# A hybrid encoder block on one core: the second copy of the keys made in the memory-attention stage, and five units instead of seven woven with the grouped-query attention

## The chip, the core and the metric

The kernel runs on one core of a Trainium2 chip. The metric is device time in microseconds, the median over runs. The engines are named as in the profile: PE is TensorE's matrix multiplication and PEld its weight load, DVE is VectorE, ACT is ScalarE, POOL is GpSimd, SP is SyncE, which here only issues transfers. "PSUM bank" is one of the eight accumulators of 128 x 512 float32 that matmuls write to; SBUF is the on-chip memory of 128 partitions.

## The reference, cut to what matters

One sub-layer with three mixers side by side. All inputs are float32, 1024 tokens, width 1024.

```python
h = rms_norm(x, g_pre[layer])
a_qkv, bq, bk, bv, mq, ga, gb, gm, mg = jnp.split(h @ w_in[layer], split_at, axis=-1)
# 1. dilated window attention: 3 groups of 8 heads, merged by their log-denominators -> oa
# 2. grouped-query attention: 8 query heads, 2 key heads of width 64
qb_ = axial_rope(rms_norm(bq, q_norm), row_pos, col_pos)
kb_ = axial_rope(rms_norm(bk, k_norm), row_pos, col_pos)
sc = jnp.einsum('bqkgd,bskd->bkgqs', qc, kb_).astype(jnp.float32) * (HEAD_DIM ** -0.5)
p = jax.nn.softmax(sc, axis=-1)
ob = jnp.einsum('bkgqs,bskd->bqkgd', p, vb_)
# 3. cross-attention of 4 heads of width 128 into a memory of 256 tokens -> om
ya = (oa * jax.nn.silu(ga)) @ w_br_a[layer]
yb = (ob * jax.nn.silu(gb)) @ w_br_b[layer]
ym = (om * jax.nn.silu(gm)) @ w_br_m[layer]
gates = jax.nn.sigmoid(mg + b_merge[layer])   # 3 x 1024 columns of the same h @ w_in
merged = gates[:, :, 0] * ya + gates[:, :, 1] * yb + gates[:, :, 2] * ym
x = x + rms_norm(merged @ w_out[layer], g_post[layer])
```

## The kernel before

**Precision and units.** A float32 product is made of three matmuls in a rounded float32 format: each operand is split into a high and a low part (`split`, lines 104 to 106: ACT writes the high part, DVE the remainder), and high x high, low x high and high x low are summed in PSUM. The normalised input stands in SBUF as `hh[k]`, `hl[k]` for eight blocks of 128 input channels. The columns of `w_in` that give transposed outputs are cut into units of 128: `add_unit` (line 195) queues one, `load_w` (line 110) loads its 512 KB of weights on SP and splits them, and `dense` (line 139) runs 2 halves x 8 channel blocks x 3 = 48 matmuls of 128 x 512 (lines 143, 145, 147). What is done with the result differs: `add_gate` (line 216) makes a SiLU gate of a branch and stores it to `g2d`; `add_filler` (line 207) makes tanh of one of the 24 merge-gate units and stores it to `thd`.

**Weaving.** The order on PE is written out: `weave` (line 174) alternates the matmuls of queued units with the pieces of an attention generator, in proportion to the costs that both announce with `yield`. While an item runs, the next one is prepared (weights loaded and split). On ACT, DVE, POOL and SP the tile scheduler chooses the order in most stages, by priority and by when its own model thinks operands are ready; each engine then runs its list strictly in that order. `tc.issue_after(x)` keeps an instruction behind another one.

**The stages in order of time.** Loading and splitting the input, keys and values of the grouped-query branch; memory keys and values; the memory-attention stage (`m_att`, about 98 to 217 us), woven with the query projection (`b_q`), the four memory-query units and one gate unit; the grouped-query stage (`b_att`, 217 to 462 us), woven with the units that this change counts; the values of the window attention in seven block products; the window attention (592 to about 1003 us), woven with its own query and key units and four gate units (`GATES_A`); the block stage (1011 to 1220 us), in which the remaining merge-gate units are made in pairs; then the three branch products and the output.

**The grouped-query stage.** `KS` holds the two key heads transposed, key on 64 rows, high part in rows 0 to 63 and low part in rows 64 to 127. `QH` holds the queries' high part in both halves, so `KS` x `QH` over 128 rows gives high x high and low x high at once. The third product takes `QL`, the queries' low part in rows 0 to 63 and, in rows 64 to 67, the row maximum of one of four heads on a diagonal; its partner is `KB`: the keys' high part again in rows 0 to 63 and -1 in rows 64 to 67, so the same matmul subtracts the maximum. The steps, for 8 query blocks x 2 key heads = 16 rounds of 8 steps:

- `q_prep` (line 661), every second round: four transposes of the normalised queries into one PSUM bank, four ACT copies to `QH`, two DVE subtractions to `QL`, which release the bank.
- `row_max` (line 713), one a step: a matmul of 128 x 512 and a DVE reduction (line 721). Its banks, three of them, also serve `q_prep`, `shift` and `final`.
- `shift` (line 725): the maxima transposed and put into `QL` (DVE, line 729).
- `scores` (line 732), 12 steps behind `row_max`: two matmuls (738 and 739), the exponential on ACT (741), the running sum of denominators on POOL (743, 745).
- `pv` (line 748), once a round, 14 steps behind: 16 matmuls with the values (754), ACT and DVE evacuations (756, 757), and the split of the finished sum into `lh`, `ll` (the profile calls them `blh`, `bll`).
- `final` (line 760), 15 steps behind: two matmuls of a column of ones with `blh` and `bll`, copied out by ACT (766) and stored.

`b_const` (line 683) is called in step 1: it makes `KB` and clears two small tiles. `token_block` (692), in steps 18, 42, 66 and 90, prepares sums of input blocks for later stages.

The woven units are the gate units (2,3) and (1,0) to (1,3), five, and `FILL_B = (16, 17)`, two merge-gate units. Line 823 prepares the first value weights for the next stage behind the last unit.

**The block stage.** `rest` (line 1344) lists the merge-gate units that are not in `FILL_B`, in the order 16 to 23, 8 to 15, 0 to 7, and `pairs` takes them by two: 11 pairs before. A pair is a 2 x 2 block product made with seven products instead of eight (`PRODUCTS`, line 1426), each 4 x 3 = 12 matmuls of 128 x 512: 84 for a pair, where two units alone have 96. `slot` (line 1528) puts the other engines' work behind each product, among it the five steps of `combine` for the last head pair, at products of pairs 0 to 4 (`COM`, line 1526); results are stored to `thd` from the ACT queue (line 1466). `last` is the number of the last pair, and the loads for the branch products count from it.

**SBUF.** `KS` and the values lie in a pool that lives through both attention stages; `QN`, the queries, in pool `qn`, opened before the memory-attention stage and closed after the grouped-query one. `mt` holds the memory attention's tiles and `ba` those of the grouped-query stage; both begin behind `qn`. A tile that reuses memory waits for the last user of the tile that lay there.

Of the kernel before, what the change touches and what calls it, by code (L numbers as in the profile page):

```python
# [8 lines left out]
F32 = mybir.dt.float32  # L9
R = mybir.dt.float32r  # L10
AF = mybir.ActivationFunctionType
# [4 lines left out]
S = 1024  # L16
NT = 8
P = 128
# [32 lines left out]
def block(ctx: ExitStack, tc: tile.TileContext, x, xT, memT, cst, msk, bcst, tabA, gpost,  # L51
          wu, wv, wb, wmem, wbr, wout, out):
    nc = tc.nc
    V, A, G, PE = nc.vector, nc.scalar, nc.gpsimd, nc.tensor
# [24 lines left out]
    def pss1():  # L79
        return bank["p"].tile([P, 512], F32, name="s1", tag="s1", bufs=bank["n"][1])  # L80

    def pst():
        return bank["p"].tile([P, 4, 128], F32, name="tr", tag="t", bufs=bank["n"][2])

    def pso():
        return bank["p"].tile([P, 512], F32, name="ov", tag="o", bufs=bank["n"][3])
# [6 lines left out]
    ones = const.tile([P, 1], F32, name="ones")  # L93
# [10 lines left out]
    def split(dst_h, dst_l, src):  # L104
        A.activation(dst_h, src, AF.Copy)  # L105
        V.tensor_tensor(dst_l, src, dst_h.bitcast(F32), op=OP.subtract)  # L106
# [3 lines left out]
    def load_w(src, n=1024):  # L110
        if extra:
            extra.append(extra.pop(0))
        raw = (extra[0] if extra else wp).tile([P, 1024], F32, name="wr", bufs=WR)
        nc.sync.dma_start(raw[:, :n], src)
        wh = wp.tile([P, 1024], R, name="wh")
        wl = wp.tile([P, 1024], R, name="wl")
        split(wh[:, :n], wl[:, :n], raw[:, :n])
        k = n // 128
        return (wh[:, :n].rearrange("p (k f) -> p k f", k=k),
                wl[:, :n].rearrange("p (k f) -> p k f", k=k))  # L120

    def passes(out_ps, terms):
        n = len(terms)
        for i, (a, b) in enumerate(terms):
            PE.matmul(out_ps, a, b, start=i == 0, stop=i == n - 1)  # L125
# [37 lines left out]
    def run_items(count):  # L163
        for _ in range(count):
            n = done[0]
            prepare(n)
            prepare(n + 1)
            yield from queue[n][1](ready.pop(n))
            done[0] += 1

    def cost_items(count):
        return sum(q[2] for q in queue[done[0]:done[0] + count])

    def weave(count, att=None, att_cost=0.0, lead=1.0, prio=ATT_PRIO):
        dg = run_items(count)
        dc = cost_items(count)
        d = a = 0.0
        live_d, live_a = True, att is not None
        while live_d or live_a:
            if live_d and (not live_a or a / att_cost >= min(1.0, d / dc * lead)):  # L180
                try:
                    d += next(dg)
                except StopIteration:
                    live_d = False
                    d = 1e18
            else:
                try:
                    with tc.high_priority(offset=prio):
                        a += next(att)
                except StopIteration:  # L190
                    live_a = False
# [11 lines left out]
    fp = {}  # L203
# [32 lines left out]
    def pool(name, side="left"):  # L236
        p = tc.tile_pool(name=name, bufs=1, side=side, reuse_waits="tile")
        return p, p.__enter__()
# [8 lines left out]
    KS = kvl.tile([P, 2, S], R, name="KS")  # L247
# [50 lines left out]
    def proj_tok(w, T, dst):  # L298
        th, tl = w
        t = slice(T * 128, T * 128 + 128)  # L300
        for k in range(8):
            PE.matmul(dst, hh[k][:, t], th[:, k], start=k == 0, stop=False)
            yield 109
            PE.matmul(dst, hl[k][:, t], th[:, k], start=False, stop=False)
            yield 109
            PE.matmul(dst, hh[k][:, t], tl[:, k], start=False, stop=k == 7)
            yield 109
# [122 lines left out]
    def b_q(c, w):  # L430
        for T in range(NT):
            p = psd() if T % 2 else pss1()
            yield from proj_tok(w, T, p[:, 0:256])
            qk_norm_rope(p, 4, T, tabs["Cq"], tabs["Sq"], -0.125, QN[T][:, 4 * c:4 * c + 4])

# [125 lines left out]

    qp, ql_ = pool("qn")
    QN = [ql_.tile([P, 8, 64], F32, name=f"qn{T}") for T in range(NT)]
    mtp, mt_ = pool("mt")
    fp["p"] = mt_

    def m_att(h):
        qh, ql = MQ[h]
        for _ in range(4):
            yield 250  # L570
        st = {}

        def scores(n):
            sv = pss1().rearrange("p (t k) -> p t k", t=2)
            nm = mt_.tile([P, 2], F32, name="mnm", bufs=3)
            l = mt_.tile([P, 2], F32, name="mls", bufs=3)
            pm = mt_.tile([P, 2, 256], F32, name="pm", bufs=2)
            for j in range(2):
                t = slice((2 * n + j) * 128, (2 * n + j) * 128 + 128)
                passes(sv[:, j], [(qh[:, t], kmh[:, h]), (qh[:, t], kml[:, h]), (ql[:, t], kmh[:, h])])  # L580
            V.tensor_reduce(nm, sv, axis=AX.X, op=OP.min)
            V.tensor_tensor(nm, nm, rcol[:, 2 * n:2 * n + 2], op=OP.mult)
            for j in range(2):
                A.activation(pm[:, j], sv[:, j], AF.Exp, scale=nrcol[:, 2 * n + j:2 * n + j + 1], bias=nm[:, j:j + 1],
                             accum_out=l[:, j:j + 1])
            rl = mt_.tile([P, 2], F32, name="mrl", bufs=4)
            V.reciprocal(rl, l)
            for j in range(2):
                V.tensor_scalar(pm[:, j], pm[:, j], rl[:, j:j + 1], None, op0=OP.mult)
            st[n] = pm  # L590

        def trans(n):
            pm = st[n]
            tp = pst().rearrange("p (k t) q -> p k t q", k=2)
            for kt in range(2):
                for j in range(2):
                    PE.transpose(tp[:, kt, j, :], pm[:, j, kt * 128:kt * 128 + 128], ident)
            ph = mt_.tile([P, 2, 256], R, name="mph", bufs=2)
            pl = mt_.tile([P, 2, 256], R, name="mpl", bufs=2)
            split(ph, pl, tp.rearrange("p k t q -> p k (t q)"))  # L600
            st[n] = (ph, pl)

        def pv(n):
            ph, pl = st.pop(n)
            o = pso()
            terms = []
            for kt in range(2):
                terms += [(vmh[:, kt, h], ph[:, kt]), (vmh[:, kt, h], pl[:, kt]), (vml[:, kt, h], ph[:, kt])]
            passes(o[:, 0:256], terms)
            om = mt_.tile([P, 256], F32, name="om", bufs=2)  # L610
            A.activation(om, o[:, 0:256], AF.Copy)
            nc.sync.dma_start(od[2, h, :, n * 256:n * 256 + 256], om)

        for n in range(7):
            if n < 4:
                scores(n)
            yield 654
            if 0 <= n - 2 < 4:
                trans(n - 2)
            yield 436  # L620
            if 0 <= n - 3 < 4:
                pv(n - 3)
            yield 654
# [7 lines left out]
    add_gate(2, 2)  # L631
    early[len(queue)] = lambda: load_w(wu[U_G + 11])
    weave(1)
    weave(2, m_att(0), M_COST, 1.2)
    weave(2, m_att(1), M_COST, 1.2)
    weave(1, m_att(2), M_COST, 1.0)
# [20 lines left out]
    with tc.tile_pool(name="ba", bufs=1, reuse_waits="tile") as ba:  # L657
# [3 lines left out]
        def q_prep(T):  # L661
# [4 lines left out]
            for j in range(4):  # L666
                PE.transpose(tp[:, j, :], QN[T][:, 2 * j:2 * j + 2].rearrange("p a b -> p (a b)"), ident)
            for e in range(2):
# [4 lines left out]
                a = slice(e * 64, e * 64 + 64)  # L673
                V.tensor_tensor(QL[0:64, e], tp[a], QH[a, e].bitcast(F32), op=OP.subtract)

        KB = ba.tile([P, 2, S], R, name="KB")
        QQ[0] = (ba.tile([P, 8, 128], R, name="QH", bufs=2), ba.tile([P, 8, 128], R, name="QL", bufs=2))
        lh = ba.tile([P, 512], R, name="blh")
        ll = ba.tile([P, 512], R, name="bll")
# [1 line left out]
        one = ba.tile([P, 1], R, name="one")  # L681
        nmt = [ba.tile([P, 68], F32, name=f"bnm{i}") for i in range(2)]
        def b_const():
            with tc.issue_after(fp["copy"].ins):
                A.activation(KB[64:68], ones[64:68, :, None].to_broadcast([4, 2, S]), AF.Copy, scale=-1.0)
            with tc.issue_after(fp["last"].ins):
                V.tensor_copy(KB[0:64], KS[0:64].bitcast(F32))
            G.tensor_copy(one, ones)
            for t in nmt:
                V.memset(t, 0.0)  # L690
# [18 lines left out]
        def b_att():  # L709
# [22 lines left out]
            def scores(i, kt):  # L732
# [5 lines left out]
                PE.matmul(s, KS[:, kv, t], QH[:, h], start=True, stop=False)  # L738
                PE.matmul(s, KB[0:68, kv, t], QL[0:68, h], start=False, stop=True)  # L739
                pp = ba.tile([P, 512], F32, name="bp", bufs=BP)  # L740
# [74 lines left out]
        for i in (2, 1, 0):  # L815
            for p_ in range(4):
                if (i, p_) not in ((2, 0), (2, 1), (2, 2)) + GATES_A:
                    add_gate(i, p_)
                    ng += 1
        for j in FILL_B:  # L820
            add_filler(j)
# [198 lines left out]
    with tc.tile_pool(name="aa", bufs=1, reuse_waits="tile") as aa:  # L1020
# [322 lines left out]

        rest = [j for i in (2, 1, 0) for j in range(8 * i, 8 * i + 8) if j not in FILL_B]
        pairs = list(zip(rest[::2], rest[1::2]))
# [43 lines left out]
        for n in range(len(seq)):  # L1389
# [6 lines left out]
            last = n + 1 == len(seq)  # L1396
# [30 lines left out]
    last = len(pairs) - 1  # L1427
# [318 lines left out]
G_AT = 4  # L1746
ATT_PRIO = 120
LA_T, LA_P = 2, 3
FILL_B = (16, 17)
GATES_A = ((0, 0), (0, 1), (0, 2), (0, 3))  # L1750
VG = (2, 0, 1)
U_G = 24
# [107 lines left out]
```

## Time and profile before

| | us |
|---|---|
| median of 3 runs (1448.71, 1448.78, 1450.25) | 1448.78 |
| the profiled execution, by the device's own time | 1449.86 |
| its span, from first to last instruction | 1448.1 |
| grouped-query stage, first row maximum to the next stage's first matmul | 245 |
| TensorE's granted clock, mean | 0.998 |

The page's first part gives the busy time of each engine, its share of the span and its number of instructions. Views by stretch give, for each stretch, its length and then busy time and instruction count of PE, PEld, DVE, ACT and POOL, the granted clock, the share of the DMA engines that was busy, and GB/s. Groups by line give engine, operation, written and read tile, shape and count, then busy time and mean length, then the idle time in front of them and what ended it. In order of time, a row gives start and length in us, and in brackets how long the engine had stood idle and what released it. Matmuls overlap: one of 512 columns is shown with about 0.39 us, and the distance from one start to the next is what it costs. A name such as `bp` or `fth` stands for all buffers of that tile.

### The profile page before, as it was taken

Reading aid. Unit: us, or ns where it says so; the run is one execution under the profiler, and the core shown is the slowest. Engines: PE = TensorE matmul, PEld = TensorE weight load, DVE = VectorE, ACT = ScalarE, POOL = GpSimd, SP = SyncE. Lnnn points to the kernel's source line nnn. Section 1 sums busy time; section 2 is a strip of 40 time slices with the busy share of each in tenths; the row PEclk is TensorE's granted clock in tenths of the full one; section 3 lists DMA queues with packets and bytes.
Section 4 is the critical chain, followed back from the end, with each engine's and each line's share of the span. In section 5 each row is a group of like instructions: output and inputs, shape, how many; then the busy total and the mean of one; then the engine's idle time right before and its main releaser. Section 6 shows DMA issues by size and latency. Waiting matters only on the chain.

```text
span 1448.1 us, 20924 instructions
## 1 busy us (share of the span) xinstructions
PE 1420.2 (98%) x7548; PEld 1138.7 (79%) x7548; DVE 986.6 (68%) x1739; ACT 642.2 (44%) x1441; POOL 500.4 (35%) x382
## 2 busy tenths in 40 slices
PE   7999999999999999999999999999999999999998
PEld 7899986565666888878778777778777888888887
DVE  7765468776762357786696786863878787559643
ACT  6544355665654253254445445554443444223231
POOL 0415504666674420232233241320324331044322
PEclk9999999999999999999999999999999999999999
DMA  6332022232111675411132132343444443767122
GB/s 232 109 117 74 16 66 91 81 98 82 55 52 48 249 226 179 139 48 43 47 98 79 45 103 62 92 129 88 140 146 138 175 174 111 285 207 281 46 88 102
DMA packets 99448, 168.05 MB, mean 116 GB/s; under 512 B 21968, under 2 KB 51856, under 8 KB 99344
## 3 DMA queue, kind: packets, MB, share of 16 engines
q1 hardware_dynamic: 80192, 148.76, 31.9%
q10 hardware_dynamic: 19152, 17.96, 3.7%
q8 instruction: 59, 0.97, 0.3%
q14 instruction: 45, 0.37, 0.1%
HBM read 124.38 MB, written 42.30 MB: 115 GB/s over the span
## 4 chain that ended last, share of the span: by engine, by line
PE 78%; DVE 6%; ACT 5%; issue 4%; POOL 3%; DMA 3%; ACTq 0%; SPq 0%; POOLq 0%; DVEq 0%
PE d L145 9%; PE sc L125 9%; PE d L147 9%; PE d L143 9%; PE s L125 8%; PE s L967 6%; PE sc L1708 5%; PE ov L754 3%; PE tr L1186 2%; PE d L967 2%; PE s L1123 2%; PE s L738 2%; PE tr L720 2%; PE s L739 2%; PE d L535 2%
## 5 line engine op out<-in xcount | busy, mean ns | idle before, releaser
L143 PE MATMUL d<-hh,wh 128*128 128x512 f32 x672 | 269.7, 401 | 0.5 <-DVE fth L222 0.5
L145 PE MATMUL d<-hl,wh 128*128 128x512 f32 x672 | 268.0, 399 | 0.0
L147 PE MATMUL d<-hh,wl 128*128 128x512 f32 x672 | 267.9, 399 | 0.0
L105 ACT ACTIVATE wh<-wr 128x1024 fp32r<-128x1024 f32 (+1 forms) x79 | 72.2, 917 | 210.3 <-PE d L145 115.0
L145 PEld LDWEIGHTS d<-hl,wh 128*128 128x128 f32 x672 | 126.5, 188 | 31.1 <-issue 8.4
L143 PEld LDWEIGHTS d<-hh,wh 128*128 128x128 f32 x672 | 126.5, 188 | 30.1 <-issue 4.9
L745 POOL TENSOR_TENSOR bl<-bl,bp 128x512 f32<-128x512 f32 x96 | 131.5, 1369 | 53.6 <-ACT bp L741 48.1
L147 PEld LDWEIGHTS d<-hh,wl 128*128 128x128 f32 x672 | 126.5, 188 | 28.4 <-issue 4.7
L125 PE MATMUL sc<-hh,wh 128*128 128x512 f32 x384 | 118.4, 389 | 0.0
L1056 POOL TENSOR_TENSOR aq<-t1a,t2a 128x512 f32<-128x512 f32 x24 | 45.4, 1893 | 171.0 <-DVE t1a L1050 161.6
L721 DVE TENSOR_REDUCE bn<-tr 128x1 f32<-128x512 f32 x128 | 86.0, 685 | 17.3 <-PE tr L720 15.9
L106 DVE TENSOR_TENSOR wl<-wr,wh 128x1024 fp32r<-128x1024 f32 x53 | 75.0, 1417 | 32.0 <-ACT wh L105 31.6
L741 ACT ACTIVATE bp<-s 128x512 f32<-128x512 f32 x128 | 75.9, 595 | 46.8 <-PE s L739 45.8
L1056 POOL TENSOR_TENSOR ak<-t1a,t2a 128x512 f32<-128x512 f32 x24 | 55.5, 2313 | 106.9 <-DVE t1a L1049 106.9
L1049 DVE TENSOR_TENSOR t2a<-d,tab 32x512 f32<-32x512 f32 x96 | 66.0, 687 | 37.7 <-PE d L147 36.4
L1435 POOL TENSOR_TENSOR sf<-wr 128x512 f32<-128x512 f32 x22 | 30.5, 1407 | 162.3 <-DVE ch L106 62.2
L125 PEld LDWEIGHTS sc<-hh,wh 128*128 128x128 f32 x384 | 72.1, 188 | 15.0
L1050 DVE SCALAR_TENSOR_TENSOR t2a<-d,tab 32x512 f32<-32x512 f32 x96 | 66.0, 687 | 26.2 <-PE d L147 24.6
L1639 POOL TENSOR_TENSOR acc<-acc,th 128x1024 f32<-128x1024 f32 x15 | 40.9, 2728 | 110.8 <-DVE th L1638 108.0
L125 PE MATMUL sc<-hl,wh 128*128 128x512 f32 x192 | 74.7, 389 | 0.0
L1143 ACT ACTIVATE pra<-pra,sts 128x128 f32<-128x128 f32 (+2 forms) x152 | 66.4, 438 | 13.4 <-DVE sts L1135 13.3
L1135 DVE CUSTOM_DVE_ANT_0 pra<-s,mask 128x192 f32<-128x192 f32 (+2 forms) x192 | 55.7, 347 | 15.8 <-PE s L1123 14.9
(375 smaller groups left out, 3435.5 us busy)
## 6 DMA issues: line engine op xcount, KB each, us to landing
wr<-in_wu SPq DMA_DIRECT2D x64, 512.0 KB
th<-thd SPq DMA_DIRECT2D x24, 512.0 KB
thd<-rs ACTq DMA_DIRECT2D x44, 256.0 KB
g2d<-fth SPq DMA_DIRECT2D x24, 256.0 KB
vdr<-vr ACTq DMA_DIRECT2D x24, 256.0 KB
wgt<-wgd SPq DMA_DIRECT2D x24, 256.0 KB
ot<-od SPq DMA_DIRECT2D x12, 512.0 KB
wr<-in_wbr SPq DMA_DIRECT2D x24, 256.0 KB
```

The costliest lines, as they stand in the source:

```text
L105: A.activation(dst_h, src, AF.Copy)
L106: V.tensor_tensor(dst_l, src, dst_h.bitcast(F32), op=OP.subtract)
L125: PE.matmul(out_ps, a, b, start=i == 0, stop=i == n - 1)
L143: PE.matmul(dst, wh[:, k, :], hh[k][:, t], start=k == 0, stop=False)
L145: PE.matmul(dst, wh[:, k, :], hl[k][:, t], start=False, stop=False)
L147: PE.matmul(dst, wl[:, k, :], hh[k][:, t], start=False, stop=k == 7)
L721: fp["last"] = V.tensor_reduce(st[i]["n"][:, j, c:c + 1], s, axis=AX.X, op=OP.min)
L741: A.activation(pp, s, AF.Exp, scale=-1.0)
L745: G.tensor_tensor(lsum[i % 2], lsum[i % 2], pp, op=OP.add)
L967: PE.matmul(now[j], a, b, start=k == 0 and q == 0, stop=k == end and q == 2)
L1056: G.tensor_tensor(half_of(o, half, g), classes(t1, g), classes(t2, g), op=OP.add)
L1708: PE.matmul(parts[h], *terms[h][j], start=j == 0, stop=j == 23)
```

## The change

Three edits. `KB` becomes a tile of pool `qn`, so it lives from the beginning of the memory-attention stage. Its two instructions leave `b_const`, with the two `issue_after` that held them behind the first query copy and a row maximum, and are written behind the first memory-query unit (`weave(1)`), one DVE copy and one ACT instruction for each key head; the scheduler places them from there. `FILL_B` becomes empty: the two merge-gate units are no longer woven with the grouped-query attention, and `rest` has 24 units and so 12 pairs, of which the first is now (16, 17).

```diff
     QN = [ql_.tile([P, 8, 64], F32, name=f"qn{T}") for T in range(NT)]
+    KB = ql_.tile([P, 2, S], R, name="KB")
     mtp, mt_ = pool("mt")
...
     weave(1)
+    for kv in range(2):
+        V.tensor_copy(KB[0:64, kv], KS[0:64, kv].bitcast(F32))
+        A.activation(KB[64:68, kv], ones[64:68].to_broadcast([4, S]), AF.Copy, scale=-1.0)
     weave(2, m_att(0), M_COST, 1.2)
...
-        KB = ba.tile([P, 2, S], R, name="KB")
         QQ[0] = (ba.tile([P, 8, 128], R, name="QH", bufs=2), ba.tile([P, 8, 128], R, name="QL", bufs=2))
...
         def b_const():
-            with tc.issue_after(fp["copy"].ins):
-                A.activation(KB[64:68], ones[64:68, :, None].to_broadcast([4, 2, S]), AF.Copy, scale=-1.0)
-            with tc.issue_after(fp["last"].ins):
-                V.tensor_copy(KB[0:64], KS[0:64].bitcast(F32))
             G.tensor_copy(one, ones)
...
-FILL_B = (16, 17)
+FILL_B = ()
```

## The prediction

> **What bounds the kernel now.** I read the page's first part, then the busy times by stretch, because the change takes matmuls from one stage and gives them to another: the question is which engine ends each of the two.
>
> ```profile
> span 1448.1 us, 20924 instructions
> PE 1420.2 (98%) x7548; PEld 1138.7 (79%) x7548; DVE 986.6 (68%) x1739; ACT 642.2 (44%) x1441; POOL 500.4 (35%) x382
> ```
>
> TensorE is busy for 98% of the span, so in a stretch where it is the bound a matmul taken out is worth one slot of it. The grouped-query stage runs from about 217 to 462 us. The next fence shows its opening, three of its 16 rounds (from the start of one value product, L754, to the next) and the sum over the whole stage; columns are PE, weight loads, DVE, ACT and POOL busy time with instruction counts, then clock and DMA.
>
> ```profile
> 217.10:229.20 12.10, 10.02 (x42) 7.17 (x43) 11.79 (x22) 5.96 (x6) 0.00 (x0) 1.00 0.44 152
> 254.70:270.24 15.54, 15.00 (x64) 8.85 (x65) 11.40 (x18) 10.59 (x18) 10.08 (x8) 1.00 0.24 77
> 285.04:299.41 14.37, 14.37 (x65) 9.30 (x66) 12.09 (x19) 8.02 (x14) 9.50 (x7) 1.00 0.24 83
> 343.30:358.49 15.19, 14.52 (x64) 8.99 (x65) 11.40 (x19) 10.55 (x18) 9.27 (x7) 1.00 0.26 86
> sum 245.38, PE 242.04 PEld 155.48 DVE 169.50 ACT 143.61 POOL 153.08; mean PE 13.45 PEld 8.64 DVE 9.42 ACT 7.98 POOL 8.50
> ```
>
> In an ordinary round (285 to 299) TensorE is full. In two rounds it is not (0.54 and 0.67 us idle, and 15.54 and 15.19 us long instead of 14.37), and at the start DVE is the full engine: 11.79 of 12.10 us. So TensorE is the bound by a small margin: DVE has 12.09 us of work in a round of 14.37. Who waits for whom in the rounds, from 229.2 us on:
>
> ```profile
> L745 POOL TENSOR_TENSOR bl<-bl,bp 128x512 f32<-128x512 f32 x96 | 131.5, 1369 | 53.6 <-ACT bp L741 48.1
> L721 DVE TENSOR_REDUCE bn<-tr 128x1 f32<-128x512 f32 x116 | 78.5, 686 | 17.1 <-PE tr L720 15.8
> L106 DVE TENSOR_TENSOR bll<-bl,blh 128x512 fp32r<-128x512 f32 x16 | 11.5, 716 | 34.8 <-ACT blh L105 34.7
> L105 ACT ACTIVATE blh<-bl 128x512 fp32r<-128x512 f32 x16 | 10.0, 627 | 33.7 <-POOL bl L745 33.7
> ```
>
> POOL sums the exponentials one after another; ACT stands 33.7 us, 2.1 us a round, at `blh` until that sum is done, and DVE 34.7 us behind ACT. These waits cost nothing as long as TensorE has other matmuls to run. The units woven in are those matmuls.
>
> **Term 1, the units leave the stage.** Seven units of 48 matmuls become five: 96 fewer, six in each round. One slot, from the order in time on TensorE:
>
> ```profile
> 243.54 0.39 PE L143 MATMUL d<-hh,wh 128*128 128x512 f32 x1
> ...
> 244.69 0.39 PE L147 MATMUL d<-hh,wl 128*128 128x512 f32 x1
> ...
> 246.56 0.40 PE L720 MATMUL tr<-KS,QH 128*128 128x512 f32 x1
> ...
> 248.90 0.40 PE L738 MATMUL s<-QH,KS 128*128 128x512 f32 x1
> ```
>
> The first pair is five slots apart (0.230 us each), the second ten slots with attention matmuls between (0.234). I take 0.232: 96 x 0.232 = 22.3 us off, 1.4 us a round, if TensorE stays the bound. With them go four stores and two weight loads from the SP queue, and on DVE and ACT each four evacuations and two splits; SP, DVE and ACT only get emptier.
>
> **Term 2, they come back as a twelfth pair.** A pair of units is seven products of twelve matmuls in the block stage: 84 for 96. Three ordinary pairs and a slow one:
>
> ```profile
> 1069.35:1089.70 20.35, 19.62 (x86) 15.61 (x84) 17.13 (x19) 7.39 (x11) 5.61 (x4) 1.00 0.43 130
> ...
> 1129.90:1148.94 19.04, 19.04 (x85) 15.77 (x84) 14.56 (x19) 7.38 (x11) 6.40 (x4) 1.00 0.51 177
> 1148.94:1167.98 19.04, 19.04 (x85) 15.77 (x84) 15.80 (x21) 7.38 (x11) 6.40 (x4) 1.00 0.53 181
> 1167.98:1187.02 19.04, 19.04 (x85) 15.77 (x84) 15.81 (x20) 7.57 (x12) 6.39 (x4) 1.00 0.52 189
> ```
>
> The slow pairs are those that carry or follow a step of the last head pair's combination, and these steps stay at pairs 0 to 4; the added pair is a plain one. TensorE is full there, so its two loads on SP, four stores on the ACT queue and its splits (DVE 15.8 of 19.04) lie beside it. +19.0 us; if it came out slow, 20.35. Terms 1 and 2 together are -3.3 us, the most that the moved units can give. [...]
>
> **Term 3, the start of the stage.** On TensorE, DVE and ACT:
>
> ```profile
> 217.72 0.50 PE L720 MATMUL tr<-KS,QH 128*128 128x512 f32 x1 [1.00 <-ACT QH L671]
> 220.46 0.47 PE L720 MATMUL tr<-KS,QH 128*128 128x512 f32 x1 [0.62 <-DVE QL L674]
> 222.94 0.50 PE L720 MATMUL tr<-KS,QH 128*128 128x512 f32 x1 [0.85 <-DVE bn L721]
> ```
>
> ```profile
> 221.06 1.22 DVE L687 CAST KB<-KS 64x2048 fp32r<-64x2048 f32 x1
> 222.21 4.26 DVE L721 TENSOR_REDUCE bn<-tr 128x1 f32<-128x512 f32 x7
> ```
>
> ```profile
> 218.91 1.91 ACT L685 ACTIVATE KB<-ones 4x2048 fp32r<-4x2048 f32 x1
> 223.35 2.44 ACT L697 ACTIVATE tx<-tx,cs 128x1024 f32<-128x1024 f32 x2 [2.53 <-DMA tx<-in_xT]
> 229.26 0.59 ACT L670 ACTIVATE QH<-tr 64x512 fp32r<-64x512 f32 x1 [3.48 <-PE tr L667]
> ```
>
> The 1.22 us cast stands in front of seven reductions, and a row maximum waits 0.85 us for them; the constant rows on ACT hold up nobody (ACT waits for a load next). Without the cast the reductions move up by 1.22 us, and DVE, nearly full here, sets the pace: the start shortens by 1.2 us. But the 42 matmuls here are 13 row maxima, 4 transposes, one shift and 24 of units, and two sevenths of these, 7, are in term 1 with 1.6 us. So +0.4 us against term 1; bounds: -0.8 (the 0.85 us goes on top) and +1.6 (nothing gained). The tiles of the memory attention now lie 8 KB higher, so the `tx` loads may have to wait for a gate store; ACT is idle for 3.48 us before its next need, which hides that: 0.
>
> **Term 4, the same work earlier.** The copy and the rows become two halves each (DVE about 0.61, ACT about 0.95 us) after the first memory-query unit, when the keys are complete:
>
> ```profile
> 85.20:98.50 13.30, 13.30 (x70) 11.31 (x69) 6.12 (x9) 4.80 (x7) 0.00 (x0) 1.00 0.52 158
> 98.50:110.00 11.50, 11.50 (x101) 11.50 (x99) 7.63 (x24) 3.56 (x11) 7.57 (x14) 1.00 0.01 1
> ```
>
> TensorE is full, DVE works 6.12 and ACT 4.80 of 13.30 us: both fit in idle time. Behind them wait only splits and evacuations that have this slack. 0; if they fell on evacuations that TensorE waits for, 1.22 + 1.91 = +3.1. [...]
>
> **Term 5, the rounds.** What the other engines need does not shrink by 1.4 us a round. In some rounds `blh` comes on ACT ahead of the four copies of the next queries, in others behind them:
>
> ```profile
> 256.31 0.63 ACT L105 ACTIVATE blh<-bl 128x512 fp32r<-128x512 f32 x1 [3.88 <-POOL bl L745]
> ```
>
> ```profile
> 344.59 0.63 ACT L105 ACTIVATE blh<-bl 128x512 fp32r<-128x512 f32 x1 [3.55 <-POOL bl L745]
> 375.04 0.62 ACT L105 ACTIVATE blh<-bl 128x512 fp32r<-128x512 f32 x1
> ```
>
> The first two open the stalls of the two long rounds: ACT idles 3.88 and 3.55 us with the query copies queued behind it, the copies hold one of three PSUM banks, the row maxima wait. That chain runs over POOL, ACT and DVE and holds no dense matmul, so those two rounds keep most of their length and give back up to 1.4 us each; in the other rounds a few tenths in all. I take +2.5. Bounds: -2.0 (a new order frees both rounds: 15.54 + 15.19 - 2 x 14.37) and +9.8 (all seven rounds with a query preparation stall: 7 x 1.4). I am near the low end because in five of seven the copies come first.
>
> **Term 6, the end of the stage.** The last sum and the two matmuls that need it:
>
> ```profile
> 459.83 0.69 DVE L106 TENSOR_TENSOR bll<-bl,blh 128x512 fp32r<-128x512 f32 x1 [9.71 <-ACT blh L105]
> ```
>
> ```profile
> 460.70 0.40 PE L125 MATMUL tr<-blh,one 128*1 128x512 f32 x1
> 460.93 0.40 PE L125 MATMUL tr<-bll,one 128*1 128x512 f32 x1
> ```
>
> `bll` is done at 460.52 and needed at 460.93: 0.4 us to spare. In the last round some 26 dense matmuls stand before that point; 7 fewer bring TensorE there 1.7 us sooner, while POOL's chain, whose second exponential waits for 2 of them, gains only 0.5. A stall of 1.7 - 0.5 - 0.4 = +0.8 us; 0 to 1.7. Next late is the value stage's first load, which SP issues behind the reciprocal of the last sums:
>
> ```profile
> 467.92 0.84 SPq L858 DMA_DIRECT2D sum<-in_wv  x2
> ```
>
> It is tied to the last sum, and after it TensorE has one or two dense matmuls less before the stage that uses it: +0.3; 0 to 0.9.
>
> **Sum.** -22.3 + 19.0 + 0.4 + 0 + 2.5 + 0.8 + 0.3 = +0.7 us. The profiled execution took 1449.86 us around its span of 1448.1, 1.1 above the median: 1450.6 for a like execution, and for the median 1448.78 + 0.7 = **1449.5 us**. I call a change real from 0.2%, 2.9 us: below 1445.9 or above 1451.7.
>
> **Rivals.** *Faster:* TensorE stays full throughout. For it: 14.37 us rounds without idle, and at most 12.09 us of work on any other engine where 13.0 remain. Against: both long rounds, the full DVE at the start, 0.4 us to spare at the end. Terms 1 and 2 alone: 1445.5; with the long rounds cured 1443.5. *Slower:* the order on ACT, which nobody wrote by hand and which follows the new spacing, puts `blh` ahead of the query copies in five to seven of the seven rounds. It decides from the fourth such round on: 7.0 to 9.8 us in place of 2.5 makes +5.2 to +8.0, 1454.0 to 1456.8. For it: POOL's 9.5 us a round do not shrink, so `blh` comes later against TensorE; against: today it is two of seven. *The copy in the wrong place:* +3.1 from term 4, 1452.6; against it stands the slack in both fences. *The copy does not move in time:* it has no pinned place and could still be run late, which leaves the start as it is: +1.2, 1450.7, inside the forecast.
>
> **How the numbers follow.** Forecast, 1446 to 1452: 0.52. Faster: 0.17. Slower by the order on ACT: 0.24. Copy in the wrong place: 0.07. The range for eight in ten leaves out the cured rounds and the worst of the slow case: 1445.2 to 1455.0. Faster by over 0.2% is the first rival, 0.17; slower holds the two others and the top of the forecast, 0.33; within 0.2% the rest, 0.50. Cases of both signs hold less than the forecast; its own range is 1446.5 to 1451.5.
>
> **What would show it.** Right: the stage about 18.6 us shorter (227 for 245.4), TensorE idle in it some 3 us more than the 3.3 of before, two or three rounds with a row maximum waiting behind `QL`, the block stage longer by 19.0, no TensorE wait between 85 and 110 us. Wrong: the stage shorter by 22 us or more; or by less than 16, with `blh` waits ahead of the query copies in most rounds; or a new wait in the memory attention.

## The result and the profile after

The changed kernel takes 1455.83 us (median of 6 runs, 1454.09 to 1456.70), the kernel before 1448.82 (6 runs, 1448.36 to 1450.25): slower by 0.44%, ratio 1.0044 with a 95% interval of 1.0032 to 1.0057. The forecast of 1449.5 us and its range up to 1455.0 both missed. The profiled execution took 1454.75 us around a span of 1452.9; against the profile before (1449.86) that is +4.9 us of the +7.0 between the medians. The tables below thus explain an execution of the changed kernel a little faster than the typical one, against one of the kernel before that is 1.0 us slower than its median.

The span split by the first matmul of each part, in us:

| stretch | before | after | difference |
|---|---|---|---|
| up to the first row maximum | 217.72 | 216.80 | -0.9 |
| start: first row maximum to first value product | 21.90 | 25.68 | **+3.8** |
| the 15 distances between value products | 215.54 | 198.46 | -17.1 |
| last round | 7.16 | 7.08 | -0.1 |
| values of the window attention | 156.05 | 157.40 | +1.4 |
| window attention | 391.50 | 391.74 | +0.2 |
| block stage, 11 and 12 pairs | 214.10 | 231.68 | +17.6 |
| branches and output | 224.10 | 224.10 | 0 |

The busy times by stretch of before and then of after carry the start (after its length: PE, PEld, DVE, ACT and POOL busy with counts, granted clock, DMA share, GB/s):

```profile
217.72:239.62 21.90, 20.39 (x85) 14.31 (x85) 20.32 (x35) 13.42 (x19) 6.83 (x6) 1.00 0.25 85
```

```profile
216.80:242.48 25.68, 20.18 (x75) 14.03 (x75) 19.59 (x34) 11.41 (x18) 7.96 (x7) 0.87 0.21 72
...
242.48:440.94 198.46, 196.42 (x852) 121.20 (x852) 144.65 (x215) 123.07 (x207) 139.43 (x103) 1.00 0.21 68
```

Ten matmuls fewer, and yet 3.8 us more; TensorE idles 5.5 us where it idled 1.5, and its mean clock, 1.00 before, is 0.87. In order of time, DVE and then TensorE of after show the place, and the chain of waits names it:

```profile
216.97 0.12 DVE L689 MEMSET bnm<- 128x68 f32 x1
221.46 0.12 DVE L689 MEMSET bnm<- 128x68 f32 x1 [4.38 <-DMA g2d<-fth]
221.49 0.65 DVE L720 TENSOR_REDUCE bn<-tr 128x1 f32<-128x512 f32 x1
```

```profile
216.80 0.50 PE L719 MATMUL tr<-KS,QH 128*128 128x512 f32 x1 [1.23 <-ACT QH L675]
222.29 0.77 PE L719 MATMUL tr<-KS,QH 128*128 128x512 f32 x1 [4.30 <-DVE bn L720]
```

```profile
by line: DMA g2d<-fth 35.7%; PE tr L719 17.0%; DVE wl L106 10.2%; ACT wh L105 8.0%; PE d L143 7.1%; DVE fth L222 5.0%; DVE bn L720 4.8%; PE d L145 3.6%; PE d L147 3.5%; ACT om L612 3.2%; issue 2.3%; DVE bnm L689 1.2%; DVEq L689 0.2%
...
217.04 4.29 DMA g2d<-fth
```

The clearing of the second `bnm` tile waits 4.38 us for a store of `fth`, the last gate buffer of the stage before, to land; the first reduction is queued behind it and TensorE stands for 4.30 us.

Three rounds are long as well. Below are these three by stretch, then an ordinary round with a query preparation and an ordinary one without, of 13 unit matmuls each:

```profile
255.90:270.60 14.70, 13.96 (x59) 8.10 (x58) 12.01 (x19) 10.17 (x17) 10.26 (x9) 1.00 0.28 98
270.60:285.06 14.46, 13.69 (x61) 8.39 (x60) 11.51 (x15) 8.18 (x14) 8.24 (x7) 1.00 0.33 102
285.06:299.37 14.31, 13.79 (x59) 8.13 (x58) 11.70 (x18) 8.51 (x15) 10.37 (x9) 1.00 0.13 46
299.37:312.79 13.42, 13.42 (x61) 8.47 (x60) 9.80 (x17) 8.71 (x14) 9.08 (x7) 1.00 0.28 89
312.79:325.77 12.98, 12.98 (x58) 8.17 (x57) 12.26 (x19) 9.91 (x17) 9.37 (x8) 1.00 0.41 131
```

ACT in two of them:

```profile
259.62 1.15 ACT L696 ACTIVATE tx<-tx,cs 128x1024 f32<-128x1024 f32 x1 [1.05 <-DMA tx<-in_xT]
...
277.10 1.15 ACT L696 ACTIVATE tx<-tx,cs 128x1024 f32<-128x1024 f32 x1 [2.21 <-DMA tx<-in_xT]
```

The scaling of a token block stands on ACT before its load has landed, with exponentials queued behind it. The query copies, by contrast, stand ahead of `blh` in all seven preparations of this profile.

The rest is as planned. The copy of the keys runs near 90 us, with TensorE full around it and POOL without work, and the added pair is a plain one:

```profile
90.40 1.28 DVE L636 CAST KB<-KS 64x1024 fp32r<-64x1024 f32 x2
92.56 2.00 ACT L637 ACTIVATE KB<-ones 4x1024 fp32r<-4x1024 f32 x2
```

```profile
85.20:98.50 13.30, 13.30 (x73) 11.47 (x72) 6.83 (x9) 5.86 (x9) 0.00 (x0) 1.00 0.52 159
...
1190.76:1209.80 19.04, 19.04 (x85) 15.77 (x84) 15.86 (x20) 7.79 (x12) 6.40 (x4) 1.00 0.38 128
```

### The profile page after: what moved, and what is told of

Same layout as the page of the kernel before. It is cut to its first block, busy times and chain, and to the rows that moved or that the text cites. A ratio compares the mean times of both kernels' runs of the same rounds, so it can differ in the third digit from the quotient of the medians.

```text
span 1452.9 us, 20930 instructions
## 1 busy us (share of the span) xinstructions
PE 1419.4 (98%) x7536; PEld 1136.0 (78%) x7536; DVE 997.5 (69%) x1751; ACT 645.3 (44%) x1447; POOL 504.9 (35%) x386
## 4 chain that ended last, share of the span: by engine, by line
PE 83%; DVE 6%; ACT 4%; issue 3%; DMA 2%; POOL 2%; ACTq 0%; SPq 0%; POOLq 0%; DVEq 0%
PE s L125 14%; PE sc L125 9%; PE d L145 9%; PE d L147 9%; PE d L143 9%; PE s L966 6%; PE sc L1707 5%; PE ov L753 3%; PE tr L1185 2%; PE d L966 2%; PE s L738 2%; PE s L737 2%; PE tr L719 2%; PE s L1122 2%; PE d L535 2%
## 5 line engine op out<-in xcount | busy, mean ns | idle before, releaser
L143 PE MATMUL d<-hh,wh 128*128 128x512 f32 x640 | 257.4, 402 | 2.6 <-DVE fth L222 1.7
L147 PE MATMUL d<-hh,wl 128*128 128x512 f32 x640 | 256.0, 400 | 0.0
L145 PE MATMUL d<-hl,wh 128*128 128x512 f32 x640 | 255.5, 399 | 0.0
L143 PEld LDWEIGHTS d<-hh,wh 128*128 128x128 f32 x640 | 120.8, 189 | 31.7 <-issue 5.1
L145 PEld LDWEIGHTS d<-hl,wh 128*128 128x128 f32 x640 | 120.8, 189 | 29.6 <-issue 7.6
L147 PEld LDWEIGHTS d<-hh,wl 128*128 128x128 f32 x640 | 120.8, 189 | 26.9 <-issue 5.0
L720 DVE TENSOR_REDUCE bn<-tr 128x1 f32<-128x512 f32 x128 | 85.5, 684 | 14.4 <-PE tr L719 12.8
L1434 POOL TENSOR_TENSOR sf<-wr 128x512 f32<-128x512 f32 x24 | 33.8, 1428 | 172.4 <-DVE ch L106 73.0
L1464 ACT ACTIVATE rs<-rs,hbm 128x512 f32<-128x512 f32 x48 | 34.6, 721 | 80.7 <-DVE rs L1463 80.7
```

The costliest lines, as they stand in the source:

```text
L143: PE.matmul(dst, wh[:, k, :], hh[k][:, t], start=k == 0, stop=False)
L145: PE.matmul(dst, wh[:, k, :], hl[k][:, t], start=False, stop=False)
L147: PE.matmul(dst, wl[:, k, :], hh[k][:, t], start=False, stop=k == 7)
L720: fp["last"] = V.tensor_reduce(st[i]["n"][:, j, c:c + 1], s, axis=AX.X, op=OP.min)
```

## The experiments

All times are medians; each kernel is compared with runs of the kernel before on the same chip, which lay between 1448.88 and 1449.13 us.

| run | units woven | us | ratio to before, 95% | start, us | 15 distances, us |
|---|---|---|---|---|---|
| e1, clearing on POOL | 5 | 1455.65 | 1.0046 [1.0033, 1.0058] | 25.76 | 198.3 |
| e2, copy moved alone | 7 | 1454.81 | 1.0037 [1.0023, 1.0051] | 26.91 | 215.5 |
| e3, units moved alone | 5 | 1452.55 | 1.0025 [1.0015, 1.0035] | 22.42 | 198.33 |
| e4, e2 with clearing on POOL | 7 | 1454.36 | 1.0036 [1.0024, 1.0049] | 26.83 | 215.6 |
| e5, tiles away from the store | 5 | 1451.57 | 1.0020 [1.0010, 1.0029] | 21.20 | 198.29 |
| e6, e5 with seven units | 7 | 1448.79 | 1.0000 [0.9991, 1.0008] | 20.72 | 215.38 |
| e7, e5 with `tx` later | 5 | 1449.58 | 1.0005 [0.9996, 1.0013] | 21.19 | 196.15 |
| e8, e6 with `tx` later | 7 | 1449.22 | 1.0004 [0.9995, 1.0013] | 20.70 | 216.14 |
| e9, e7 with a denser start | 5 | 1455.52 | 1.0045 [1.0032, 1.0057] | 20.90 | 201.52 |
| e10, e9 with a denser end | 5 | 1447.97 | 0.9991 [0.9982, 1.0000] | 19.95 | 195.79 |
| e11, e9 with `blh` pinned | 5 | 1450.38 | 1.0007 [0.9998, 1.0016] | 20.92 | 196.91 |
| e12, e6 with `blh` pinned | 7 | 1447.00 | 0.9985 [0.9977, 0.9994] | 20.72 | 213.77 |

**The two halves, and a first guess at the wait.** e1 is the changed kernel, e4 the copy alone, each with this edit; e2 is the changed kernel with `FILL_B = (16, 17)`, e3 the kernel before with `FILL_B = ()`.

```diff
-                V.memset(t, 0.0)
+                G.memset(t, 0.0)
```

> The changed kernel with one edit: the two small tiles bnm are cleared by POOL instead of DVE, at the same addresses and with the same wait for the gate store. My theory: DVE's 4.38 us wait at the second clearing, with all reductions queued behind it, is what made the start of the grouped-query stage 25.7 us (first row maximum to first value product) instead of 21.9; on POOL, which has nothing to do before 234 us, the same wait costs nothing. Expected: that stretch 20.5 to 21.5 us, median 1451 to 1452. Rival, the start is slow because units are missing and DVE is the bound there: the stretch stays above 24.5 us and the median at 1455 to 1456.

> The kernel before with the copy and the constant rows moved to the memory-attention stage, and FILL_B still (16, 17). My theory: the move alone brings the wait at the clearing, since it is the move that shifts the tiles by 8 KB; first row maximum to first value product 24.5 to 26 us, median 1451 to 1453, slower than before. Rival, the move only takes 1.2 us off DVE at the start: the stretch 20.7 us, median 1447.6.

> The kernel before with FILL_B empty, the copy where it was. My theory: no wait at the clearing; terms 1 and 2 give -3.3, the start stays at about 21.5 to 22 (7 fewer unit matmuls, +1.6 against term 1, because DVE sets its pace), three early rounds are 0.7 to 1.5 us too long (+3), the end +0.3: 1450 to 1451. Rival, the missing units are the whole loss: 1455 to 1456.

> The kernel before with the copy moved and the clearing on POOL, FILL_B still (16, 17). My theory: the start is 1.2 us shorter than before and nothing else moves: 1447.3 to 1448.0, the best of the four. Rival, the copy at 90 us or its tiles cost something else: 1448.8 or more.

Each half alone is slower: the copy by 5.8 us, of which the profile shows 5.0 at the start (26.91 against 21.90 us), the units by 3.6. The two do not add up to the 7 of the whole change, because the start behind the wait takes 26.9 us with seven units and 25.7 with five. It may be that the ten matmuls that the units take from the start do count there, since TensorE is late; but with seven units the half clock described in the last section also lasts longer, 6.6 us behind the wait instead of 3.9, and no run separates the two.

All four missed what was expected of them: e2 and e3 in size, 1.8 and 1.6 us above the top of their ranges, and e1 and e4, with the clearing on POOL, in kind. The DVE rows of these two tell why; first e1, then e4:

```profile
221.87 0.69 DVE L720 TENSOR_REDUCE bn<-tr 128x1 f32<-128x512 f32 x1 [4.40 <-DMA g2d<-fth]
```

```profile
221.95 0.69 DVE L720 TENSOR_REDUCE bn<-tr 128x1 f32<-128x512 f32 x1 [4.32 <-DMA g2d<-fth]
```

With the clearing gone from DVE the reduction itself waits for the same store, just as long. So it was not one instruction in the way: `bn`, where the reductions write, waits for the gate buffer too.

**All small tiles away from the store.** e5 is the changed kernel with this edit, e6 the same with seven units:

```diff
     KB = ql_.tile([P, 2, S], R, name="KB")
+    nmt = [ql_.tile([P, 68], F32, name=f"bnm{i}") for i in range(2)]
+    bn2 = [ql_.tile([P, 4, 2], F32, name=f"bn{i}") for i in range(2)]
...
-        nmt = [ba.tile([P, 68], F32, name=f"bnm{i}") for i in range(2)]
...
-                    st[i] = dict(n=ba.tile([P, 4, 2], F32, name="bn2", bufs=2))
+                    st[i] = dict(n=bn2[i % 2])
```

> The changed kernel with the two running-minimum tiles bnm and the two row-minimum tiles bn of the grouped-query attention placed in the pool of the normalised queries, where no gate store of the stage before reads; nothing is left out. My theory: the 3.8 us that the start lost is the wait of the first reductions for the store of the last gate buffer, whose place they took. Then the first row maximum no longer waits 4.4 us for it, the stretch from first row-maximum matmul to first value matmul goes from 25.7 to 20.7-22.4 us, the rest stays, and the time is 1451.0-1452.6 us. Rival: the store only stands where another dependency of the same length would (another tile lands on the buffer, or the stage has to wait for its loads anyway): stretch 25 or more, 1455-1456 us.

> The run before with seven units instead of five in the grouped-query stage, so the copy alone is moved and the twelfth pair is not added. My theory: start stretch 20.7-22.4 us as there, rounds, last round, value stage and block stage as before the change, so 1447.5-1449.2 us: at or up to 1.3 us under the kernel before. Rival (the move costs something besides the overlap with the store): 1451 us or more.

DVE of e5 at the same place, the store still issued at 218.10:

```profile
217.39 0.68 DVE L222 SCALAR_TENSOR_TENSOR fth<-d,fth 128x512 f32<-128x512 f32 x1
218.40 0.69 DVE L721 TENSOR_REDUCE bn<-tr 128x1 f32<-128x512 f32 x1 [0.33 <-PE tr L720]
```

The wait is gone, the start takes 21.20 us, and the time falls by 4.3 us from the changed kernel's 1455.83 (by 6.0 from e2 to e6). The rival, another wait of the same length behind it, falls. With seven units the moved copy is then worth nothing that can be measured (1448.79 against 1448.88), though its start is 1.2 us shorter than before; where that is lost is open.

**The long rounds.** e7 and e8 order the scaling of the later three token blocks behind the exponentials:

```diff
-                A.activation(t, t, AF.Copy, scale=cs[:, C_GP + k + 4 * j:C_GP + k + 4 * j + 1])
+                with tc.issue_after(fp["exp"].ins) if k else ExitStack():
+                    A.activation(t, t, AF.Copy, scale=cs[:, C_GP + k + 4 * j:C_GP + k + 4 * j + 1])
...
-                A.activation(pp, s, AF.Exp, scale=-1.0)
+                fp["exp"] = A.activation(pp, s, AF.Exp, scale=-1.0)
```

> The first run of this set with the scaling of the later three token blocks (tx, ScalarE) ordered behind the exponentials that stand ahead of it in the program, instead of where its load is due. Theory A: in the three long rounds (255.9-299.4 us, 43.5 us in all where 13 or 14 unit matmuls each need about 39.8) ScalarE stands at tx for a load (2.2 us in one place) with exponentials behind it; without that they take 41.3-42.6 us and the time is 1.0-2.2 us under the first run of this set. Theory B: the loss there is VectorE, whose instructions with two inputs take 1.3-2.3 us beside GpSimd instead of 0.7-1.2: the rounds stay at 43.2-43.8 us and the time within 0.5 us of the first run.

> The second run of this set (seven units) with the same later tx. With seven units two rounds are long in the kernel before (15.47 and 15.15 us where 18 unit matmuls make about 14.1). Theory A: these shorten by 1-2 us in all and the time is 1446-1448 us. Theory B: unchanged rounds, time within 0.5 us of the second run.

The three rounds by stretch, e5 and then e7:

```profile
252.50:267.28 14.78, 13.98 (x58) 8.04 (x57) 11.98 (x19) 10.12 (x17) 10.26 (x9) 1.00 0.30 99
267.28:281.75 14.47, 13.70 (x61) 8.40 (x60) 11.52 (x15) 8.17 (x14) 8.23 (x7) 1.00 0.33 101
281.75:296.02 14.27, 13.71 (x58) 8.13 (x57) 11.69 (x18) 8.51 (x15) 10.35 (x9) 1.00 0.13 46
```

```profile
253.21:266.72 13.51, 13.51 (x58) 8.20 (x57) 11.75 (x19) 9.31 (x16) 9.16 (x8) 1.00 0.39 128
266.72:280.11 13.39, 13.39 (x62) 8.56 (x61) 10.22 (x15) 8.35 (x14) 10.27 (x9) 1.00 0.27 90
280.11:294.51 14.40, 13.84 (x59) 8.13 (x58) 11.72 (x18) 8.92 (x16) 9.64 (x8) 1.00 0.13 46
```

Two of the three become full rounds of TensorE, 43.52 us become 41.30, and the time falls by 2.0 us: theory A's number. The longest wait of TensorE in each of these rounds in the changed kernel, and a DVE row in front of the third:

```profile
268.27 0.50 PE L719 MATMUL tr<-KS,QH 128*128 128x512 f32 x1 [0.56 <-DVE bn L720]
278.93 0.50 PE L737 MATMUL s<-QH,KS 128*128 128x512 f32 x1 [0.77 <-ACT bp L740]
297.05 0.50 PE L719 MATMUL tr<-KS,QH 128*128 128x512 f32 x1 [0.52 <-DVE bn L720]
```

```profile
295.02 1.37 DVE L702 TENSOR_TENSOR tb<-tx 128x512 f32<-128x512 f32 x1
```

In the second round TensorE waits for an exponential, and those stand behind `tx` on ACT: that is theory A. In the first and the third it waits for a reduction, which on DVE stands behind a subtraction `tb` of 1.37 us beside POOL (0.68 at its shortest, also beside POOL): the long DVE instruction of theory B, though POOL alone does not explain its length (last section). e7 frees the first round too, but there DVE's busy time changes as well, with the same number of instructions: from 11.98 to 11.75 us in the first round and from 11.52 to 10.22 in the second; so for the first round the way is not separated. The third stays at 14.4 us with the same wait for DVE (0.56 us in e7), and no run tests it. With seven units the same edit gains nothing: theory B's number, because the two long rounds there have another cause (below).

**Where TensorE is not the bound.** e9 and e10 change only how densely the units are woven at the two ends: `START_PAD` from 700 to 1300, and in e10 also `END_PAD` from 300 to 700.

> The run with tiles away from the store and later tx, five units, START_PAD 1300 instead of 700: the weave then puts 34 instead of 26 unit matmuls into the stretch from the first row maximum to the first value matmul, and 193 instead of 201 into the rounds. Theory: that stretch is set by VectorE and by the lags, not by TensorE (20.72 us with 36 unit matmuls, 21.19 with 26), so the ten that the change took from there gave nothing back. The stretch then stays at 20.7-21.7 us, the rounds fall from 196.2 to 194.0-194.8 us (8 x 0.232 = 1.9 off), and the time is 1447.2-1448.6 us. Rival: the rounds are held by the other engines by now and the stretch grows with its matmuls: time 1449-1450.5 us, as without it.

> As the run before it, and END_PAD 700 instead of 300: 33 unit matmuls in the first stretch, 191 in the rounds, 12 instead of 9 behind the last value product. Theory: three more leave the rounds (-0.7 us) and stand where TensorE waits 0.5 us for the split of the last sum, so the last stretch stays within 0.3 us of its 7.06; time 0.2-1.0 us under the run before it. Rival: the last stretch grows by 3 x 0.232 and the time stays the same.

The start behaves as the theory said: 34 unit matmuls in 20.90 us (33 in 19.95 in e10) where 26 took 21.19. But e9 as a whole missed by 7 us: its rounds became longer, not shorter. Two of them, and ACT in the first:

```profile
307.00:322.21 15.21, 13.73 (x58) 7.94 (x57) 10.70 (x17) 10.83 (x18) 9.63 (x9) 1.00 0.24 78
335.71:351.27 15.56, 13.96 (x57) 7.84 (x56) 11.39 (x17) 8.98 (x16) 10.29 (x9) 1.00 0.23 76
```

```profile
309.00 0.63 ACT L105 ACTIVATE blh<-bl 128x512 fp32r<-128x512 f32 x1 [4.76 <-POOL bl L746]
309.53 0.58 ACT L676 ACTIVATE QH<-tr 64x512 fp32r<-64x512 f32 x1
...
312.60 0.59 ACT L677 ACTIVATE QH<-tr 64x512 fp32r<-64x512 f32 x1
```

This is the order that the prediction's slow rival described: `blh` ahead of the query copies, in two of seven preparations; TensorE's longest waits in these two rounds, 1.38 and 1.03 us, are for the `QL` that needs the copies. e10, which differs by one number, has this order in none. It was expected 0.2 to 1.0 us under e9 and came 7.5 under it, so it missed as well. Two last runs put the order to the test, e9 (as e11) and e6 (as e12) with

```diff
-                split(lh, ll, lsum[i % 2])
+                with tc.issue_after(fp["copy"].ins):
+                    split(lh, ll, lsum[i % 2])
```

> The run with the denser start (1455.5 us; rounds of 14.43, 15.21, 13.50, 15.56 and 14.53 us from the fifth to the ninth, where 13 unit matmuls need 13.0 and, with a query preparation, 13.4) with one line more: the split of the finished sum (blh) is ordered behind the query copies written before it. In the dense-start run two of the seven preparations came behind a blh that waits 4.76 and 3.83 us for GpSimd; here none does. Theory (the order on ScalarE, the prediction's slow rival, is what made that run slow): those five rounds fall from 73.2 to 67.0-69.5 us, the first round (15.12) stays, and the time is 1449.5-1452.0 us. Rival (the order does not matter; the weave of units against attention does): rounds unchanged, time 1454.5-1456.5 us.

> The run with seven units and tiles away from the store (1448.79 us) with the same line: the split of the finished sum ordered behind the query copies. With seven units two of seven preparations come behind it, as in the kernel before, in rounds of 15.50 and 15.12 us. Theory: these two become ordinary rounds, 14.3-14.8 us, and the time falls by 1.0-2.0 us to 1446.8-1447.8 us, under the kernel before. Rival (the two rounds are long for GpSimd's sum, whatever stands first): time within 0.5 us of 1448.8 us.

The same rounds in e11, then the two long ones of seven units in e6 and in e12:

```profile
308.02:321.31 13.29, 13.23 (x58) 8.10 (x57) 11.14 (x17) 9.62 (x17) 9.38 (x8) 1.00 0.30 89
334.81:347.77 12.96, 12.96 (x57) 8.13 (x56) 10.89 (x17) 7.95 (x14) 9.02 (x8) 1.00 0.29 91
```

```profile
253.42:268.92 15.50, 14.94 (x63) 8.78 (x62) 11.37 (x18) 10.59 (x18) 10.03 (x8) 1.00 0.24 77
342.04:357.16 15.12, 14.45 (x63) 8.94 (x62) 11.34 (x19) 10.55 (x18) 9.20 (x7) 1.00 0.26 87
```

```profile
253.68:268.46 14.78, 14.44 (x62) 8.95 (x62) 11.72 (x18) 9.35 (x15) 9.99 (x8) 1.00 0.25 81
341.63:355.75 14.12, 14.12 (x62) 9.10 (x61) 10.96 (x18) 9.19 (x16) 9.16 (x7) 1.00 0.29 94
```

The rounds fall by 1.92 and 2.60 us in e11 and by 0.72 and 1.00 in e12; nothing else in those kernels was edited. Inside the stage, the lists of ACT and DVE in the profiles differ only around `blh` and `bll`, in their places and in the order of the few instructions that they passed, and the lists of TensorE and POOL not at all. e11 drops from 1455.52 to 1450.38 us. Its profile shows 4.6 us of that in the rounds, and 1.1 and 0.8 in the value stage and the block stage, whose waits change from profile to profile. e12 is the one kernel of the study that is clearly under the kernel before, by 2.0 us.

## Why the prediction was wrong

**The step that failed** is in term 3: "The tiles of the memory attention now lie 8 KB higher, so the `tx` loads may have to wait for a gate store; ACT is idle for 3.48 us before its next need, which hides that: 0." The overlap and the store were seen. The wrong part is who lands there: not `tx`, which has slack, but `bn` and `bnm`, on which the whole stage waits. By the code, all of `ba` was moved relative to `mt`, because `KB` left its beginning, and the question "which tile now lies where the last store still reads" was asked of one tile instead of all. The price is not 0 but 4.5 us in the profile (25.68 - 21.20) and 4.3 in the median (1455.83 - 1451.57).

Without that wait the sum comes near, in part by luck. In e5 the stage takes 226.6 us (217.86 to 444.43), 18.0 less than the 244.6 of before on the same measure (217.72 to 462.32), where 18.6 less was predicted. Its profiled execution took 1451.27 us, 1.4 more than that of before where +0.7 was the sum; by the medians it is 2.7 slower than the kernel before (1451.57 against 1448.88), so the sum is still 2 us short. The changed kernel itself shows one of the prediction's signs of being wrong, a stage shorter by less than 16 us (231.2, so 13.4), and not the one named beside it, `blh` ahead of the query copies.

- Terms 1 and 2. The added pair costs 19.04 us, as predicted; the block stage grew by 17.6 in the changed kernel's profile and by 19.1 in e5's, the difference lying in the slow early pairs. Over all profiles it takes 213.8 to 214.9 us with 11 pairs and 231.7 to 233.3 with 12. Of the 22.3 us, 81 of the 96 matmuls were in the rounds (933 before, 852 after), 18.8 us of which 17.1 came back; ten were in the start and gave nothing, since it takes 20.72 us with seven units (e6) and 21.20 with five (e5). Four stood behind the last value product (13 before, 9 after) and gave 0.1 us; the last one lies ahead of these stretches.
- Term 3, apart from the wait: the cast's 1.2 us do come off (21.90 before, 20.72 in e6). With five units only 0.7 of it is left, while the ten slots are worth 2.3 in term 1, so the start is +1.6 us against that term where +0.4 stood. Term 5, which came out lower, made up for most of this; that is luck.
- Term 4: right, 0. No wait of TensorE between 85 and 110 us.
- Term 5: +2.5 predicted, and 1.7 lost (18.8 - 17.1), but not by the mechanism given. The order of `blh` did not turn against the changed kernel; the loss goes with the place of `tx`, 2.2 us by e7. That order is real all the same: e9, e11 and e12 show it at 0.7 to 2.6 us a round, where 1.4 was reckoned. The upper bound counted seven rounds with a query preparation; the first preparation stands before any `blh` (229.26 us, the first `blh` at 241.89), so it should have been six.
- Term 6: `blh` and `bll` are waited for by 0.18 and 0.33 us, 0.5 together, and the last round gives 0.1 us for four slots of 0.9 in all, so 0.8 is lost as predicted. In the value stage one wait of 0.92 us stands near 580 us in the profile; e1's, with the same order of units, has none, and e12's, with seven units, has the same, so I put nothing on it.

The rival that came nearest in time, the order on ACT (1454.0 to 1456.8), was right by number for the changed kernel and wrong by cause.

## What to carry to other kernels

When a tile moves between pools, list which tiles of the next stage now lie on the last buffers of the stage before, and ask of each whether something at the head of a queue needs it; a small tile on a buffer that is still being stored can stop an engine for the whole flight of the store (here DVE stood 4.38 us while the store took 4.29). A matmul taken out is worth its slot only in stretches that TensorE bounds (here 17.1 of 18.8 us in the rounds, nothing in the start); count those that lie at the ends separately. And where a scheduler chooses the order of an in-order engine, an edit elsewhere can turn it: pin the one order that the longest chain needs (`blh` behind the query copies was worth 1.8 us from e6 to e12 and 5.1 from e9 to e11), then compare variants.

## What the runs showed of the hardware

**The clock fell in the wait.** By stretch, the changed kernel's TensorE after its 4.30 us of idling, and the spacing of its matmuls:

```profile
222.29:224.00 1.71, 1.71 (x4) 1.38 (x5) 1.68 (x4) 1.28 (x2) 0.00 (x0) 0.50 0.29 117
224.00:226.00 2.00, 2.00 (x6) 1.52 (x6) 1.93 (x3) 1.02 (x1) 0.00 (x0) 0.50 0.00 0
226.00:228.00 2.00, 2.00 (x10) 1.61 (x9) 1.77 (x3) 0.00 (x0) 0.00 (x0) 0.94 0.00 0
```

```profile
222.85 0.63 PE L143 MATMUL d<-hh,wh 128*128 128x512 f32 x1
223.28 0.63 PE L145 MATMUL d<-hl,wh 128*128 128x512 f32 x1
```

In the changed kernel's trace the granted clock is 0.50 from 219.40 to 226.22 us, and in that time a matmul takes 0.43 us instead of 0.23. So the wait costs TensorE its 4.3 us and then some 1.9 us of slow matmuls (3.96 us for nine slots from 222.29 to 226.25, less 9 x 0.232), part of which DVE would have taken anyway. In e2, whose wait is 3.64 us, the mean clock is 0.98 from 216.94 to 222.24 us, 0.50 from there to 228.00 and 0.80 from 228.00 to 230.00. That puts the half clock at about 222.0 to 228.8 us: as long as the changed kernel's 6.8 us, but it falls about 3.4 us into the idling instead of 1.4, and so stays low for about 6.6 us of the matmuls behind the wait instead of 3.9.

What sets the moment of the fall and the length of the half clock was not shown. The prediction had no term for a lower clock behind any of its waits. In the traces of the kernel before and of the changed kernel, TensorE's waits of 0.85 to 1.73 us go with a clock of 1.00, but one of 2.04 us in the kernel before, which ends at 30.07 us, goes with a clock of 0.50 from 30.03 to 33.45 us.

**Some DVE instructions are longer beside POOL.** In the changed kernel, DVE and then POOL:

```profile
215.18 1.22 DVE L106 TENSOR_TENSOR wl<-wr,wh 128x1024 fp32r<-128x1024 f32 x1 [0.26 <-ACT wh L105]
...
270.29 1.72 DVE L702 TENSOR_TENSOR tb<-tx,tb 128x512 f32<-128x512 f32 x1
...
273.13 2.28 DVE L106 TENSOR_TENSOR wl<-wr,wh 128x1024 fp32r<-128x1024 f32 x1
```

```profile
264.43 7.03 POOL L744 TENSOR_TENSOR bl<-bl,bp 128x512 f32<-128x512 f32 x5 [0.17 <-ACT bp L740]
272.68 1.65 POOL L742 TENSOR_TENSOR bl<-bp 128x512 f32<-128x512 f32 x1 [1.23 <-ACT bp L740]
```

The split `wl` takes 2.28 us with POOL at work for its first 1.2 us, and 1.22 at 215.18 us, where POOL is idle. In the changed kernel's whole trace this split takes 1.22 to 1.23 us wherever POOL is idle, and 1.21 to 2.28 us where it is at work for all or part of the time. `tb` takes 1.72 us at 270.29, beside POOL for most of it; but the sixteen `tb` of the stage take 0.68 to 1.72 us, and POOL is at work for most of each, of the shortest too, so POOL's work alone does not give the length. The reductions, which read PSUM, take 0.65 to 0.69 us with POOL idle or at work. The long `wl` and the long `tb` hold DVE 1.06 and 1.04 us longer than the short ones do. A long row alone does not make a round long: in the changed kernel's round from 312.79 to 325.77 us a `wl` takes 1.85 us (at 313.99 us), and TensorE is busy for all 12.98 us.
